# Where the weight parts begin in their buffers, in a decoder layer's matmuls

## The chip, the cores and the metric

The kernel runs on one core of a Trainium2 chip. Time is device time in microseconds for one execution; three runs gave 1137.29 to 1138.82 us, median 1138.13 us. A core has five engines that run their own instruction queues and meet at semaphores: TensorE (PE, with its weight loads shown as PEld), VectorE (DVE), ScalarE (ACT), GpSimd (POOL) and SyncE (SP), which issues most DMAs. SBUF is the memory on the chip that all of them read, with 128 partitions (rows); PSUM takes what TensorE computes.

## The reference

One layer of a decoder: 256 tokens, width 2,048, sixteen heads of 128 in two groups, an MLP of 8,192. All is float32.

```
h = rms_norm(x, norm1_g)
q_a, k_a, v_a, f_a, q_b, k_b, v_b = split(h @ w_in)          # 2048 x 6152
y_a = fox_attention(q_a, k_a, v_a, log_sigmoid(f_a + forget_b))
y_b = dilated_attention(q_b, k_b, v_b, rel_bias)
mixed = concatenate(rms_norm(y_a, outnorm_a_g), rms_norm(y_b, outnorm_b_g))
x = x + mixed @ w_out                                         # 2048 x 2048
h = rms_norm(x, norm2_g)
x = x + square(relu(h @ w_mlp_in)) @ w_mlp_out                # 2048 x 8192, 8192 x 2048
return rms_norm(x, final_norm_g)
```

## The kernel before

**Split operands.** A float32 value is kept as two parts of type float32r, hi (the value as ScalarE's copy rounds it) and lo (what remains, subtracted on VectorE). A product is three matmuls: hi by hi, hi by lo, lo by hi. Weights are split as they arrive (`split_rows`, L171 and L172), activations as they leave PSUM (`split_psum`, and L242/L243 with a gain).

**Chunks and steps.** All weights are cut into chunks of 512 columns: twelve for the projection ("q", "v", "k" of four groups of heads), eight for the output projection ("o", two kinds by four columns, each over 1,024 rows), and for each of four rounds four "u" (first MLP matrix) and four "d" (second). A chunk of 2,048 rows has 16 slots, one for each 128 rows (`kt`), and 8 steps of two slots. `load` brings 512 rows of a chunk by one DMA on SP into one of four `raw` buffers; a row of such a buffer has 520 elements, because one "v" chunk brings eight columns more, the forget gates. `split` makes the parts `whi` and `wlo` of one step, two times 512 columns in a buffer of their own, three steps (`LEAD`) before TensorE needs them; there are four buffers of each.

**Two ways of multiplying.** In `product` (L302 to L304; chunks q, k, v, o, d) 128 activation columns are the stationary operand, loaded by LDWEIGHTS, and 512 weight columns move past them. In `turned_product` (L316; chunks u) 128 weight columns are stationary and 256 activation columns (`aT_hi`, `aT_lo`) move. So each slot has six matmuls of 512 columns, or twelve of 256.

**The order** is written out by hand: a loop over all steps issues loads, splits and products, and `side` holds what else runs after each slot (drains, attention, norms). Each engine runs its own queue in that order. The places where buffers matter here:

- `wf` holds the two parts of the forget-gate weights of one step of the first "v" chunk. GpSimd makes them (L161, L162) when the step is split; TensorE uses them as the stationary operand of 16 columns at the end of each slot (L336). It has four buffers. In GpSimd's queue, between these, stands the power of the first norm (L264, called from `first_norm`), which VectorE needs for `rstdq`, by which the first query chunk is drained (L453 on ScalarE, L454 on VectorE) before its transposes (L466).
- `gate_h` is the decay of one head, made by GpSimd (L476) three slots before the head's scores (L493); heads follow each other every four slots. `sqt` holds the squares of a head's values (L547 on ScalarE), added up by GpSimd (L549). Both have two buffers.
- The last chunk has no `whi` and `wlo` for its first four steps: its parts go to `aT_hi` and `aT_lo`, whose activations have been used by then.

In SBUF, all buffers of `whi`, `wlo`, `aT_hi`, `aT_lo` and of the attention's and the MLP's activations begin at a multiple of 512 bytes, and every matmul's operand begins at a multiple of 512 bytes within them; only `wf` begins at multiples of 64.

Of the kernel before, what the change touches and what calls it, by code (L numbers as in the profile page):

```python
# [11 lines left out]
F32 = mybir.dt.float32  # L12
F32R = mybir.dt.float32r
# [6 lines left out]
P = 128  # L20
D_MODEL = 2048
SEQ = 256
TB = SEQ // P
HD = 128
NH = 8
D_GRP = NH * HD
D_FF = 4 * D_MODEL
KT = D_MODEL // P
CW = 512
# [7 lines left out]
QSCALE = HD ** -0.5  # L37

LEAD = 3
WARM, WARM2 = 8, 1  # L40


# [26 lines left out]
def kernel(  # L69
# [25 lines left out]
    one = ctx.enter_context(tc.tile_pool(name="one", bufs=1))  # L95
    two = ctx.enter_context(tc.tile_pool(name="two", bufs=2))
    wraw = ctx.enter_context(tc.tile_pool(name="wraw", bufs=4))
    wsplit = ctx.enter_context(tc.tile_pool(name="wsplit", bufs=LEAD + 1))
    few = ctx.enter_context(tc.tile_pool(name="few", bufs=1))
    psum = ctx.enter_context(tc.tile_pool(name="psum", bufs=2, space=PSUM))  # L100
    dram = ctx.enter_context(tc.tile_pool(name="dram", bufs=1, space=DRAM))
# [3 lines left out]
    chunks = []  # L105
# [27 lines left out]
    def load(i):  # L133
        if i >= len(steps) or steps[i][1] % 2 or (steps[i][0], steps[i][1] // 2) in raws:
            return
        ci, s = steps[i]
        _, _, w, r0, c0, cols, _ = chunks[ci]
        t = wraw.tile([P, 4, CW + NH], F32, name="raw")
        src = w[r0 + s * 256:r0 + s * 256 + 512, c0:c0 + cols].rearrange("(k p) c -> p k c", p=P)
        raws[ci, s // 2] = t  # L140
        if i == 0:
            return t, src
        n = 2 if i == 2 else 4
        for k in range(0, 4, n):
            nc.sync.dma_start(t[:, k:k + n, :cols], src[:, k:k + n])

    def split(i, j0=0, n=2):
        if i >= len(steps):
            return
        if j0:  # L150
            return split_rows(i, j0, n)
        ci, s = steps[i]
        t = raws[ci, s // 2][:, 2 * (s % 2):2 * (s % 2) + 2, :]
        if ci == len(chunks) - 1 and s < 4:
            hi, lo = (a[:, 4 * s:4 * s + 4, :].rearrange("p (k j) s -> p k (j s)", k=2) for a in (aT_hi, aT_lo))
        else:
            hi, lo = (wsplit.tile([P, 2, CW], F32R, name=n) for n in ("whi", "wlo"))
        if chunks[ci][5] > CW:
            f = wsplit.tile([P, 2, 2 * NH], F32R, name="wf")
            fh, fl = f[:, :, :NH], f[:, :, NH:]  # L160
            nc.gpsimd.tensor_copy(fh, t[:, :, CW:])  # L161
            nc.gpsimd.tensor_tensor(fl, t[:, :, CW:], fh.bitcast(F32), op=ALU.subtract)  # L162
            forget_w[i] = f
        splits[i] = (hi, lo)
        split_rows(i, j0, n)

    def split_rows(i, j, n):
        ci, s = steps[i]
        hi, lo = (a[:, j:j + n, :] for a in splits[i])
        t = raws[ci, s // 2][:, 2 * (s % 2) + j:2 * (s % 2) + j + n, :CW]  # L170
        nc.scalar.activation(hi, t, AF.Copy)  # L171
        nc.vector.tensor_tensor(lo, t, hi.bitcast(F32), op=ALU.subtract)  # L172
# [53 lines left out]
    gT = lead_in.tile([P, 96], F32, name="gT")[:, :48]  # L226
# [3 lines left out]
        nc.tensor.transpose(p[:, :k1], grow[:k1], ident[:k1, :k1])  # L230
        nc.vector.tensor_copy(gT[:, k0:k1], p[:, k0:k1])

    aT_hi = one.tile([P, KT, SEQ], F32R, name="aT_hi")
    aT_lo = one.tile([P, KT, SEQ], F32R, name="aT_lo")

    def split_psum(hi, lo, src, scale=None):

        if scale is None:
            nc.scalar.activation(hi, src, AF.Copy)  # L239
            nc.vector.tensor_tensor(lo, src, hi.bitcast(F32), op=ALU.subtract)  # L240
        else:
            nc.scalar.activation(hi, src, AF.Copy, scale=scale)  # L242
            nc.vector.scalar_tensor_tensor(  # L243
                lo, src, scale, hi.bitcast(F32), op0=ALU.mult, op1=ALU.subtract
            )

    def to_features(kt0, gain, n=2):

        p = psum.tile([P, 512], F32, name="tr")
        for j in range(n):  # L250
            for t in range(TB):
                c = (kt0 + j) * P
                nc.tensor.transpose(p[:, j * SEQ + t * P:j * SEQ + (t + 1) * P], xs[:, t, c:c + P], ident)  # L253
        for j in range(n):
            kt = kt0 + j
            split_psum(aT_hi[:, kt, :], aT_lo[:, kt, :], p[:, j * SEQ:(j + 1) * SEQ], gT[:, gain + kt:gain + kt + 1])

    def rsqrt(dst, ssq, n):

# [46 lines left out]
    def turned_product(ci, i, j, kt, kts):  # L306


        if kt == 0:
            accs[ci] = [psum.tile([P, CW], F32, name="acc", bufs=4) for _ in range(2)]  # L310
        hi, lo = splits[i]
        terms = ((hi, aT_hi), (hi, aT_lo), (lo, aT_hi))
        for b in range(4):
            acc = accs[ci][b // 2][:, b % 2 * SEQ:(b % 2 + 1) * SEQ]
            for n, (w, a) in enumerate(terms):
                nc.tensor.matmul(acc, w[:, j, b * P:(b + 1) * P], a[:, kt, :],  # L316
                                 start=kt == 0 and b % 2 == 0 and n == 0, stop=kt == kts - 1 and n == 2,
                                 skip_group_check=True)

    def products(i, j):  # L320
        ci, s = steps[i]
        what, key, _, _, _, cols, kts = chunks[ci]
        kt = 2 * s + j
        if what == "u":
            return turned_product(ci, i, j, kt, kts)
        if kt == 0:
            accs[ci] = [psum.tile([P, CW], F32, name="acc", bufs=4) for _ in range(TB)]
            if cols > CW:
                accs["f"] = psum.tile([P, 512], F32, name="sc")
        a = operands(what, key)  # L330
        go, end = kt == 0, kt == kts - 1
        for t in range(TB):
            product(accs[ci][t], a, kt, t, splits[i], j, slice(0, CW), go, end)
        if cols > CW:
            for n, part in enumerate(a[:2]):
                nc.tensor.matmul(accs["f"][:2 * NH, :SEQ], forget_w[i][:, j], part[:, kt, :],  # L336
                                 start=go and n == 0, stop=end and n == 1)
# [4 lines left out]
    def at(i, f, *a):  # L342
        side.setdefault(i, []).append((f, a))
# [128 lines left out]
    decay = {}  # L472

    def decay_of(hd):
        decay[hd] = two.tile([P, SEQ], F32R, name="gate_h")
        nc.gpsimd.tensor_scalar(  # L476
            decay[hd], gate_t.bitcast(F32), head[:, hd:hd + 1], 1.0, op0=ALU.mult, op1=ALU.mult
        )
# [50 lines left out]
    sq = [one.tile([P, SEQ], F32, name=f"sq{k}") for k in range(2)]  # L529
    seen = [0, 0]  # L530

    def values(g, h):
        half, kind = groups[g][3:]
        hd = kind * NH + half * 4 + h
        vh, vl = qkv[g, "v"]
        ph, pl = turned.pop((g, h))
        y = psum.tile([P, 512], F32, name="sc")
        terms = ((vh, ph), (vh, pl), (vl, ph))
        for t, c0, c1, o0 in ((0, 0, SEQ, 0), (1, SEQ, 3 * P, P)):
            for n, (v, p) in enumerate(terms):  # L540
                nc.tensor.matmul(  # L541
                    y[:, o0:SEQ], v[:, t, h * P:(h + 1) * P], p[:, c0:c1],
                    start=t == 0 and n == 0, stop=t == 1 and n == 2,
                )
        first = seen[kind] == 0
        s = sq[kind] if first else two.tile([P, SEQ], F32, name="sqt")
        nc.scalar.activation(s, y[:, :SEQ], AF.Square)  # L547
        if not first:
            nc.gpsimd.tensor_tensor(sq[kind], sq[kind], s, op=ALU.add)  # L549
        split_psum(yT_hi[:, hd, :], yT_lo[:, hd, :], y[:, :SEQ], gT[:, 32 + hd:33 + hd])  # L550
        seen[kind] += 1
# [126 lines left out]
    for ci, (what, key, *_rest) in enumerate(chunks[:-1]):  # L678
# [10 lines left out]
        elif what in "qk":  # L689
# [4 lines left out]
            if what == "k":  # L694
                kind = groups[key][4]
                for h in range(4):
                    n = e + 6 + 4 * h
# [20 lines left out]

    idle_products(WARM)
    split(0, 0, 1)  # L720
    gains(0, 16)
    to_features(0, 0, 1)
    split(0, 1, 1)
    to_features(1, 0, 1)
    idle_products(WARM2)
# [13 lines left out]
    at(21, nc.vector.tensor_copy, gcat, pk[:, :2 * P].rearrange("p (t s) -> p t s", t=TB))  # L739
    ahead = 2 * LEAD + 1  # L740

# [3 lines left out]
    for i in range(final):  # L745
        if i:
            load(i + ahead)
        for k in range(done + 1, upto.get(i, i + LEAD) + 1):
            split(k)
            load(k + LEAD + 2)  # L750
            done = k
# [34 lines left out]
```

## Time and profile before

| | |
|---|---|
| median of three runs | 1138.13 us |
| the profiled execution's own time | 1138.08 us |
| its span, first to last instruction | 1136.3 us |
| mean granted TensorE clock | 0.998 |
| bytes read from HBM | 205.93 MB, 183 GB/s over the span |
| first "u" chunk begins | 409 us |

The lines by which the time is read stand in the prediction. In a line of groups or of one source line, the name behind the operation is what it writes, the arrow, and what it reads; "128x256" is partitions by elements, "x1024" how many there were. Matmuls overlap: an instruction's duration holds its passage through the array, so the pace is read from starts, or from the length of a long row of them. L numbers are lines of the kernel before.

### The profile page before, as it was taken

The numbers are of one execution on the slowest core, as the hardware profiler recorded it, in microseconds if no ns is written. First come the engines' busy times: TensorE is split into PE (matmuls) and PEld (weight loads), VectorE is DVE, ScalarE is ACT, GpSimd is POOL, SyncE is SP. The second block draws the span as 40 slices with busy tenths as digits, with TensorE's granted clock in tenths as the row PEclk, the third lists the DMA queues.
The fourth block names the chain that finished last, engine by engine and source line by source line (L and its number), as shares of the span: only waits on it lengthen the run. The fifth ranks groups of instructions, "written<-read, shape, count | busy, mean of one in ns | idle before, by whom it ended". The sixth has DMA issues, their size and how long they took to land.

```text
span 1136.3 us, 16038 instructions
## 1 busy us (share of the span) xinstructions
PE 1124.0 (99%) x6635; PEld 993.6 (87%) x6635; DVE 639.5 (56%) x795; ACT 522.0 (46%) x675; POOL 32.2 (3%) x57
## 2 busy tenths in 40 slices
PE   8999999999999999999999999999999999999996
PEld 6778888888888899998889998889998889999886
DVE  5666656556576665555555555545555544555564
ACT  5545545445445554443334444343444333454451
POOL 0110201000001000000000000000000000000000
PEclk9999999999999999999999999999999999999999
DMA  8665454554544555556665555565555566546641
GB/s 310 223 203 168 149 186 148 185 186 149 186 149 168 169 186 184 182 172 210 201 196 178 185 182 196 185 189 182 169 203 187 194 200 190 181 161 202 242 148 74
DMA packets 104933, 209.08 MB, mean 184 GB/s; under 512 B 3651, under 2 KB 4508, under 8 KB 104732
## 3 DMA queue, kind: packets, MB, share of 16 engines
q1 hardware_dynamic: 104556, 207.00, 55.4%
q8 instruction: 52, 0.85, 0.3%
q0 software_dynamic: 304, 1.06, 0.3%
q14 instruction: 21, 0.17, 0.0%
HBM read 205.93 MB, written 2.11 MB: 183 GB/s over the span
## 4 chain that ended last, share of the span: by engine, by line
PE 98%; DMA 1%; DVE 0%; SPq 0%; ACT 0%; POOL 0%; issue 0%; DVEq 0%
PE acc L316 32%; PE acc L302 21%; PE acc L304 20%; PE acc L303 20%; PE sc L496 1%; PE sc L541 1%; PE tr L466 1%; DMA raw<-in_w_in_dram 1%; PE tr L253 1%; PE tr L523 0%; PE sc L336 0%; PE sc L493 0%; DVE wlo L172 0%; ACT whi L171 0%; DVE xs L649 0%; SPq L188 0%
## 5 line engine op out<-in xcount | busy, mean ns | idle before, releaser
L172 DVE TENSOR_TENSOR wlo<-raw,whi 128x1024 fp32r<-128x1024 f32 (+1 forms) x381 | 464.0, 1224 | 377.6 <-ACT whi L171 375.3
L171 ACT ACTIVATE whi<-raw 128x1024 fp32r<-128x1024 f32 (+1 forms) x381 | 399.7, 1055 | 407.4 <-PE acc L303 238.9
L316 PE MATMUL acc<-aT_hi,whi 128*128 128x256 f32 x1024 | 289.9, 283 | 0.0
L316 PE MATMUL acc<-aT_hi,wlo 128*128 128x256 f32 x1024 | 289.8, 283 | 0.0
L316 PE MATMUL acc<-aT_lo,whi 128*128 128x256 f32 x1024 | 289.8, 283 | 0.0
L302 PE MATMUL acc<-whi,big_hi 128*128 128x512 f32 (+1 forms) x632 | 245.7, 389 | 0.0
L304 PE MATMUL acc<-wlo,big_hi 128*128 128x512 f32 (+1 forms) x632 | 244.4, 387 | 0.0
L303 PE MATMUL acc<-whi,big_lo 128*128 128x512 f32 (+1 forms) x632 | 244.4, 387 | 0.0
L316 PEld LDWEIGHTS acc<-aT_lo,whi 128*128 128x128 f32 x1024 | 196.6, 192 | 0.2
L316 PEld LDWEIGHTS acc<-aT_hi,whi 128*128 128x128 f32 x1024 | 196.6, 192 | 0.2
L316 PEld LDWEIGHTS acc<-aT_hi,wlo 128*128 128x128 f32 x1024 | 196.6, 192 | 0.0
L302 PE MATMUL acc<-whi,aT_hi 128*128 128x512 f32 x384 | 154.6, 403 | 0.0
L304 PE MATMUL acc<-wlo,aT_hi 128*128 128x512 f32 x384 | 150.2, 391 | 0.0
L303 PE MATMUL acc<-whi,aT_lo 128*128 128x512 f32 x384 | 150.1, 391 | 0.0
L304 PEld LDWEIGHTS acc<-wlo,big_hi 128*128 128x128 f32 x632 | 118.7, 188 | 24.2
L302 PEld LDWEIGHTS acc<-whi,big_hi 128*128 128x128 f32 x632 | 118.8, 188 | 23.3
L303 PEld LDWEIGHTS acc<-whi,big_lo 128*128 128x128 f32 x632 | 118.8, 188 | 23.2
L304 PEld LDWEIGHTS acc<-wlo,aT_hi 128*128 128x128 f32 x384 | 72.1, 188 | 15.7
L302 PEld LDWEIGHTS acc<-whi,aT_hi 128*128 128x128 f32 x384 | 72.2, 188 | 13.8 <-ACT fu L383 0.6
L303 PEld LDWEIGHTS acc<-whi,aT_lo 128*128 128x128 f32 x384 | 72.4, 188 | 12.9 <-DVE aT_lo L243 0.3
L240 DVE TENSOR_TENSOR big_lo<-nat,big_hi 128x512 fp32r<-128x512 f32 x32 | 22.2, 693 | 22.3 <-ACT big_hi L239 22.3
L510 ACT ACTIVATE pr<-neg,st 128x128 f32<-128x128 f32 (+1 forms) x32 | 14.3, 449 | 40.1 <-DVE st L506 40.1
(160 smaller groups left out, 532.8 us busy)
## 6 DMA issues: line engine op xcount, KB each, us to landing
raw<-in_w_mlp_in_dram SPq DMA_DIRECT2D x64, 1024.0 KB, 5.4
raw<-in_w_mlp_out_dram SPq DMA_DIRECT2D x64, 1024.0 KB, 5.2
raw<-in_w_in_dram SPq DMA_DIRECT2D x42, 1024.0 KB, 5.1
raw<-in_w_out_dram SPq DMA_DIRECT2D x16, 1024.0 KB, 5.2
raw<-in_w_in_dram SPq DMA_DIRECT2D x4, 1040.0 KB, 5.2
raw<-in_w_in_dram SPq DMA_DIRECT2D x3, 512.0 KB, 8.4
xs<-in_x_dram SPq DMA_DIRECT2D x3, 512.0 KB, 9.5
big_lo<-rel_d POOLq DMA_DIRECT2D x1, 1024.0 KB, 7.0
```

Source lines behind the costliest of these rows:

```text
L171: nc.scalar.activation(hi, t, AF.Copy)
L172: nc.vector.tensor_tensor(lo, t, hi.bitcast(F32), op=ALU.subtract)
L240: nc.vector.tensor_tensor(lo, src, hi.bitcast(F32), op=ALU.subtract)
L253: nc.tensor.transpose(p[:, j * SEQ + t * P:j * SEQ + (t + 1) * P], xs[:, t, c:c + P], ident)
L302: nc.tensor.matmul(acc, xh, hi[:, j, cols], start=go, stop=False)
L303: nc.tensor.matmul(acc, xl, hi[:, j, cols], start=False, stop=False)
L304: nc.tensor.matmul(acc, xh, lo[:, j, cols], start=False, stop=end)
L316: nc.tensor.matmul(acc, w[:, j, b * P:(b + 1) * P], a[:, kt, :], start=kt == 0 and b % 2 == 0 and n == 0, stop=kt == kts - 1 and n == 2, s ...
L466: nc.tensor.transpose(p[:, j * SEQ + t * P:j * SEQ + (t + 1) * P], ts[t][:, h * P:(h + 1) * P], ident)
L496: nc.tensor.matmul(s[:, c0:c1], q[:, h, t * P:(t + 1) * P], k[:, h, :c1 - c0], start=n == 0 and kind == 1, stop=n == 2,)
L510: nc.scalar.activation(pr[:, c0:c1], neg[:, c0:c1], AF.Exp, bias=st[:, 0, t:t + 1], scale=-1.0, accum_out=st[:, 1, t:t + 1],)
L541: nc.tensor.matmul(y[:, o0:SEQ], v[:, t, h * P:(h + 1) * P], p[:, c0:c1], start=t == 0 and n == 0, stop=t == 1 and n == 2,)
```

## The change

1. The buffers of `whi` and `wlo` get 64 elements more (`LINE`, 256 bytes). The two parts of a step begin 0 to 56 elements into their buffers, in steps of 8 elements (32 bytes); `places` gives hi's and lo's place for each chunk. Of the twelve projection chunks, the first eight have both parts at 8 times the chunk's number, the last four at two places half a line apart. The "o" chunks have lo one step after hi. Of the "u" chunks, the first eight have both parts at the same place, the others half a line apart. The "d" chunks have hi at 16 elements times the round and lo at 16 times the chunk.
2. `aT_hi` and `aT_lo` get 64 elements more and move behind the weight buffers. The first norm's activations stay at their beginning; the second norm's, which the "u" chunks use, are written and read 8 elements (32 bytes) further on (`bT_hi`, `bT_lo`).
3. `wf` has two buffers instead of four, `gate_h` and `sqt` one instead of two. With this the rest fits in memory.

All buffers still begin at multiples of 256 bytes.

```diff
+LINE = 64
...
+    wide = ctx.enter_context(tc.tile_pool(name="wide", bufs=1))
...
+    def places(ci):
+
+        what, key = chunks[ci][:2]
+        if what == "u":
+            n = 4 * key[0] + key[1]
+            return (8 * n, 8 * n) if n < 8 else (8 * (n - 8), 8 * ((n - 4) % 8))
+        if what == "d":
+            return 16 * key[0], 16 * key[1]
+        n = 4 * key[0] + key[1] if what == "o" else ci
+        if what == "o":
+            return 8 * n, 8 * ((n + 1) % 8)
+        return (8 * n, 8 * n) if n < 8 else (8 * (2 * n - 15), 8 * ((2 * n - 11) % 8))
...
-            hi, lo = (wsplit.tile([P, 2, CW], F32R, name=n) for n in ("whi", "wlo"))
+            hi, lo = (
+                wsplit.tile([P, 2 * CW + LINE], F32R, name=n)[:, b:b + 2 * CW].rearrange("p (j c) -> p j c", j=2)
+                for n, b in zip(("whi", "wlo"), places(ci))
+            )
         if chunks[ci][5] > CW:
-            f = wsplit.tile([P, 2, 2 * NH], F32R, name="wf")
+            f = wsplit.tile([P, 2, 2 * NH], F32R, name="wf", bufs=2)
...
-    aT_hi = one.tile([P, KT, SEQ], F32R, name="aT_hi")
-    aT_lo = one.tile([P, KT, SEQ], F32R, name="aT_lo")
+    aT = {}
+    for n in ("hi", "lo"):
+        aT[n] = wide.tile([P, KT * SEQ + LINE], F32R, name="aT_" + n)
+
+    def features(b):
+        return (aT[n][:, b:b + KT * SEQ].rearrange("p (k s) -> p k s", k=KT) for n in ("hi", "lo"))
+
+    aT_hi, aT_lo = features(0)
+    bT_hi, bT_lo = features(8)
...
-            split_psum(aT_hi[:, kt, :], aT_lo[:, kt, :], p[:, j * SEQ:(j + 1) * SEQ], gT[:, gain + kt:gain + kt + 1])
+            fh, fl = (aT_hi, aT_lo) if gain == 0 else (bT_hi, bT_lo)
+            split_psum(fh[:, kt, :], fl[:, kt, :], p[:, j * SEQ:(j + 1) * SEQ], gT[:, gain + kt:gain + kt + 1])
...
-        terms = ((hi, aT_hi), (hi, aT_lo), (lo, aT_hi))
+        terms = ((hi, bT_hi), (hi, bT_lo), (lo, bT_hi))
...
-        decay[hd] = two.tile([P, SEQ], F32R, name="gate_h")
+        decay[hd] = two.tile([P, SEQ], F32R, name="gate_h", bufs=1)
...
-        s = sq[kind] if first else two.tile([P, SEQ], F32, name="sqt")
+        s = sq[kind] if first else two.tile([P, SEQ], F32, name="sqt", bufs=1)
```

No engine's instructions change their order. What changes is who waits. GpSimd's queue at the first "v" chunk, before: each pair L161, L162 makes the `wf` of one step, and in brackets stand the engines or queues waited for (Pool, PE, DVE, and DMAHW for a load).

```order
L161 CAST wf<-raw 128x2x8 [waits DMAHW5_49]
L162 TENSOR_TENSOR wf<-raw,wf 128x2x8 [waits Pool_49]
L161 CAST wf<-raw 128x2x8
L162 TENSOR_TENSOR wf<-raw,wf 128x2x8 [waits Pool_49]
L161 CAST wf<-raw 128x2x8 [waits DMAHW6_49]
L162 TENSOR_TENSOR wf<-raw,wf 128x2x8 [waits Pool_49]
L264 TENSOR_TENSOR rstd_123<-rs_v,half_t 128x2 [waits DVE_49]
L161 CAST wf<-raw 128x2x8
L162 TENSOR_TENSOR wf<-raw,wf 128x2x8 [waits Pool_49]
L161 CAST wf<-raw 128x2x8 [waits DMAHW6_49,PE_49]
```

The same place of GpSimd's queue in the changed kernel, where these lines are L179, L180 and L290:

```order
L179 CAST wf<-raw 128x2x8 [waits DMAHW5_49]
L180 TENSOR_TENSOR wf<-raw,wf 128x2x8 [waits Pool_49]
L179 CAST wf<-raw 128x2x8
L180 TENSOR_TENSOR wf<-raw,wf 128x2x8 [waits Pool_49]
L179 CAST wf<-raw 128x2x8 [waits DMAHW6_49,PE_49]
L180 TENSOR_TENSOR wf<-raw,wf 128x2x8 [waits Pool_49]
L290 TENSOR_TENSOR rstd_126<-rs_v,half_t 128x2 [waits DVE_49]
L179 CAST wf<-raw 128x2x8 [waits PE_49]
L180 TENSOR_TENSOR wf<-raw,wf 128x2x8 [waits Pool_49]
L179 CAST wf<-raw 128x2x8 [waits DMAHW6_49,PE_49]
```

The wait for TensorE has moved from the fifth pair to the third, which stands ahead of the power of the first norm.

## The prediction

> **What bounds the kernel now.** I read the page's busy shares first, then the chain that ended last in order of time, then the rows of the matmul lines, and last the few microseconds around the places where the change can make somebody wait.
>
> ```profile
> span 1136.3 us, 16038 instructions
> PE 1124.0 (99%) x6635; PEld 993.6 (87%) x6635; DVE 639.5 (56%) x795; ACT 522.0 (46%) x675; POOL 32.2 (3%) x57
> PE 98%; DMA 1%; DVE 0%; SPq 0%; ACT 0%; POOL 0%; issue 0%; DVEq 0%
> ```
>
> TensorE is busy for 99% of the span and is 98% of the chain. A busy PE need not be at its peak, so the next question is how far apart its matmuls start, which the chain in order of time tells.
>
> ```profile
> 414.58 87.84 PE acc L316 x732
> 589.49 92.15 PE acc L316 x768
> ```
>
> In the MLP's first product 768 matmuls of 256 columns take 92.15 us: 120.0 ns each. Between these two pieces (502.42 to 589.49 us) lie the 384 matmuls of 512 columns of one round of the MLP's second product: 87.07 us / 384 = 226.7 ns each. The two differ by 106.7 ns for 256 columns more, so a column costs 0.417 ns, and each matmul carries **13.3 ns** over its columns, the same at both widths. Over some 6,100 matmuls that is 81 us, the only sum here that a place in memory could change. The rows by line show how steady it is:
>
> ```profile
> L316 PEld LDWEIGHTS acc<-aT_lo,whi x1024: 187/192/192, 409.2 to 1039.6; 128*128 128x128 f32 x171
> L316 PE MATMUL acc<-aT_hi,whi x1024: 277/283/365, 409.2 to 1039.6; 128*128 128x256 f32 x171
> L316 PE MATMUL acc<-aT_lo,whi x1024: 279/283/283, 409.4 to 1039.7; 128*128 128x256 f32 x171
> ...
> L303 PEld LDWEIGHTS acc<-whi,big_lo x632: 187/188/192, 310.7 to 1127.3; 128*128 128x128 f32 x158
> L303 PE MATMUL acc<-whi,big_lo x632: 283/389/397, 310.9 to 1127.4; 128*128 128x512 f32 x154, 128*128 128x256 f32 x4
> L303 PE MATMUL acc<-whi,aT_lo x384: 387/389/496, 7.1 to 310.2; 128*128 128x512 f32 x192
> ```
>
> The three figures are minimum, median and maximum in ns. Two things matter. The median is nearly the maximum, although the weight buffers, the columns of a weight and the activation rows change from matmul to matmul; but all those starts are multiples of 512 bytes, so the rows say nothing of starts in between. And a weight load that lies wholly beside a matmul of 256 columns takes 192 ns, beside one of 512 columns 188: matmul and next load do touch each other a little.
>
> **Part one, the new starts.** Nothing is added or removed on TensorE: the same 6,635 loads and matmuls in the same order, reading hi and lo weights 0 to 224 bytes into their buffers and, in the first MLP product, activations 32 bytes in. The price per matmul is not in the trace, so it is bounded by the nearest rows. From below: the shortest L316 matmul is 277 against 283, the shortest L303 one of 512 columns 387 against 389, so at best -6 and -2 ns. From above: 397 against 389, so +8 ns at 512 columns (486 and 496 are first matmuls after other work, as is the 365); at 256 columns the third L316 row goes furthest:
>
> ```profile
> L316 PE MATMUL acc<-aT_hi,wlo x1024: 278/283/285, 409.5 to 1039.8; 128*128 128x256 f32 x171
> ```
>
> 285 against 283, so +2 ns. These extremes come with changed neighbours (other matmuls just before), not with other addresses.
>
> How many would be touched? Where weights are the moving side, the start relative to the activations changes for 11 of 12 projection chunks (1,056 matmuls), 336 of the 384 of the output projection and 1,152 of the 1,536 of the second MLP product: 2,544. In the first MLP product (3,072) the moving start changes for all, the distance between the two operands for all but 320 (both parts of one chunk, hi of another, also begin 32 bytes in): 2,752. The ends are then -(2,752 x 6 + 2,544 x 2) ns = **-21.6 us** and 3,072 x 2 + 2,544 x 8 ns = **+26.5 us**.
>
> I take **0** between these ends, by three rows. First, the 13.3 ns hardly depend on how much the next load reads:
>
> ```profile
> L336 PEld LDWEIGHTS sc<-aT_hi,wf x16: 94/94/95, 35.5 to 61.1; 128*16 128x16 f32 x16
> L336 PE MATMUL sc<-aT_lo,wf x16: 277/278/281, 35.8 to 61.4; 128*16 128x256 f32 x16
> ```
>
> The forget-gate weights have 16 columns instead of 128, yet the matmul's figure falls only from 283 to 278. Two readers colliding in memory should collide an eighth as often; a fixed cost of changing weights would look like this. (These weights also begin at steps of 64 bytes, and 277 to 281 is all their spread.) Second, other readers and writers of the same memory leave no mark:
>
> ```profile
> 412.00:500.00 88.00, 88.00 (x737) 88.00 (x736) 48.48 (x54) 40.29 (x47) 0.69 (x1) 1.00 0.55 181
> ```
>
> In these 88 us (PE, PEld, DVE, ACT, POOL, clock, DMA, GB/s) VectorE is busy for 48, ScalarE for 40, the DMA engines for 55%, and the matmuls still stand 120 ns apart. Third, in one step of 120 ns a matmul reads 256 columns (1,024 bytes a row) and the next load 128 (512 bytes): wherever the two start, they drift across 512 bytes of distance in each step, and a fixed shift moves a meeting rather than removes it.
>
> The Trainium skill weighs in here: "TensorE: Matmul & The Clock Gate", Part 2, step 1, gives TensorE two independent read ports and says "Loading the next tile's weights doesn't steal SBUF read bandwidth from the running matmul." By that rule the new starts give 0; the 192 against 188 ns above does not quite agree, so the ends stay open.
>
> ScalarE and VectorE now write at those starts too. They already read at uneven ones, as a raw row is 520 elements (2,080 bytes):
>
> ```profile
> L171 ACT ACTIVATE whi<-raw x381: 629/1060/1072, 4.5 to 1109.3; 128x1024 fp32r<-128x1024 f32 x190, 128x512 fp32r<-128x512 f32 x1
> L172 DVE TENSOR_TENSOR wlo<-raw,whi x381: 692/1226/1951, 5.2 to 1110.5; 128x1024 fp32r<-128x1024 f32 x190, 128x512 fp32r<-128x512 f32 x1
> ```
>
> Median and maximum of L171 are 1% apart over all those starts, so I price the writes at 0. If they cost 10%, the cover is VectorE's 56%: nothing shows on the path.
>
> **Part two, fewer buffers.** gate_h and sqt go to one buffer. Their next writer comes four slots later (rows 6 us apart), so 0:
>
> ```profile
> 129.12 0.80 POOL L549 TENSOR_TENSOR sq<-sq,sqt 128x256 f32<-128x256 f32 x1 [5.75 <-ACT sqt L547]
> 135.35 0.74 POOL L549 TENSOR_TENSOR sq<-sq,sqt 128x256 f32<-128x256 f32 x1 [5.43 <-ACT sqt L547]
> ```
>
> GpSimd waits over 5 us before each 0.8 us of work; that is the cover.
>
> wf goes from four buffers to two, and this **adds a wait**: the third pair of wf operations may start only when TensorE has used the first wf. Behind that pair in GpSimd's queue stands the power for the first norm (L264), for which VectorE waits, with its weight splits and the first query's drain behind it.
>
> ```profile
> 27.09 0.25 POOL L161 CAST wf<-raw 128x16 fp32r<-128x16 f32 x1 [1.76 <-DMA raw<-in_w_in_dram]
> 36.36 0.72 POOL L264 TENSOR_TENSOR rstd<-rs_v,half_t 128x2 f32<-128x2 f32 x1 [8.71 <-DVE rs_v L263]
> 37.82 0.20 POOL L161 CAST wf<-raw 128x16 fp32r<-128x16 f32 x1 [0.26 <-PE sc L336]
> 38.09 1.20 POOL L162 TENSOR_TENSOR wf<-raw,wf 128x16 fp32r<-128x16 f32 x1
> 41.34 0.22 POOL L162 TENSOR_TENSOR wf<-raw,wf 128x16 fp32r<-128x16 f32 x1
> ...
> 37.11 0.16 DVE L265 TENSOR_TENSOR rs_t<-rstd 128x2 f32<-128x2 f32 x1 [0.84 <-POOL rstd L264]
> 40.30 0.74 DVE L454 TENSOR_SCALAR nat<-acc,rstdq 128x512 f32<-128x512 f32 x1
> ...
> 42.45 0.60 PE L466 MATMUL tr<-ident,nat 128*128 128x128 f32 x4
> ```
>
> The cast at 37.82 waited, with four buffers, for just that first wf's last use; with two, the cast of 27.09 waits for it. So: cast 37.82, subtraction 38.09 + 0.22 = 38.31, power until 39.05, and L265 at about 39.15 instead of 37.11: VectorE is 2.0 us late. Its splits are made three steps ahead, a step being 12 matmuls of 226.7 ns and more, so 8 us cover them. The query drain ends at 41.04 + 2.0 = 43.05, while TensorE comes for it at 42.45: **+0.6 us** on the path, with 0 and 2.0 as ends. Raw buffers come free up to 7 us later there, but loads land in 5.2 us and were waited for only twice on ScalarE:
>
> ```profile
> ACT whi L171 <- DMA raw<-in_w_in_dram: 4.2, 2, 2.3
> ```
>
> The subtraction at 38.09 took 1.20 us while VectorE ran its splits, the one at 41.34, beside none, 0.22; VectorE now stands still at that moment, so I take 0.22; with 1.20 the stall would be 1.6 us. The Trainium skill, "SBUF — State Buffer", Who interferes with whom, has a VectorE instruction with two SBUF inputs block a GpSimd one that reads SBUF; these two rows agree, and by it the small value holds here.
>
> **Sum.** The profiled execution took 1138.08 us around its span of 1136.3; the median is 1138.13, the same within 0.05. 1138.1 + 0 + 0.6 = **1138.7 us**.
>
> **Rivals.** *Faster: load and matmul collide because all starts are equal modulo 512.* For it: 192 against 188 ns, and 277 against 283 where the rhythm is broken. Against it: the 16-column row. At most -21.6 us; with half the places out of step, -10.8 + 0.6: **1127.9 us**.
>
> *Slower: a moving row that begins off a boundary needs one fetch more.* All moving starts are now even, so no row excludes it. I take it to strike starts at odd steps of 32 bytes: 768 projection and 192 output matmuls at +8 ns, 3,072 of the first MLP product at +2: 7.7 + 6.1 = 13.8 us, **1152.5 us**. It decides from about 0.4 ns per matmul: 2.3 us over 5,600.
>
> *The starts do nothing and the wf wait costs its full 2.0 us*: 1140.1, still inside the first case's bounds.
>
> **How the numbers follow.** A change within 0.2% (2.3 us) is about what a measurement of this kernel cannot tell from none. No dependence on the start, with the small wait: 0.52. Collisions lifted: 0.26. Extra fetches: 0.22. The low end, 1121, covers three quarters of the largest gain; the high end, 1153, takes in the slower case as priced; what lies past both is under 2 in 10.
>
> **What would show it.** If I am right, L316 stays at 283 and L303 at 389 in every chunk, the long L316 pieces of the chain stay at 92.15 us, and the L466 transposes near 42.5 us wait some 0.6 us for L454's line. If starts matter, pieces of the chain differ by chunk: shorter for the faster rival; longer at odd starts, with the second MLP product unchanged, for the slower one. Matmul rows that move in every chunk alike would make my reading of the 13.3 ns wrong.

## The result, and the profile after

The changed kernel takes **1144.39 us** (median of four runs, 1144.05 to 1144.53), the kernel before 1137.86 us in the four runs beside it. The ratio is 1.0056, with a 95% interval of 1.0039 to 1.0074: **slower by 6.5 us**. That is inside the predicted range, but the likeliest case, no change at 1138.7 us, is not what happened.

The page after, with the span, the busy shares, and the chain's shares:

```profile
span 1142.8 us, 16028 instructions
PE 1130.9 (99%) x6635; PEld 989.1 (87%) x6635; DVE 640.1 (56%) x795; ACT 522.0 (46%) x675; POOL 32.2 (3%) x57
PE 98%; DMA 1%; DVE 1%; SPq 0%; ACT 0%; POOL 0%; issue 0%; DVEq 0%
```

The number of matmuls and loads is the same and the chain is still TensorE's; TensorE is busy 6.9 us longer. So the time went into the pace of the matmuls. The chain in order of time splits it by stage. First the pieces of before that the prediction didn't show (start us, us, what), then those of after:

```profile
409.41 2.88 PE acc L316 x24
...
768.71 92.15 PE acc L316 x768
947.92 92.15 PE acc L316 x768
```

```profile
415.89 2.81 PE acc L342 x24
...
420.98 86.57 PE acc L342 x732
595.77 90.62 PE acc L342 x768
775.15 90.24 PE acc L342 x768
953.84 91.43 PE acc L342 x768
```

L342 is L316 of before, the first MLP product. Read both the lengths and the gaps between the pieces:

| stage | before, us | after, us | difference |
|---|---|---|---|
| up to the first MLP product (projection, attention, output projection) | 409.41 | 415.89 | +6.48 |
| first MLP product, the four long pieces | 364.29 | 358.86 | -5.43 |
| second MLP product, the three gaps between those pieces | 87.07, 87.07, 87.06 | 88.22, 88.76, 88.45 | +4.23 |
| from the last long piece to the end of the span | 96.23 | 97.53 | +1.30 |

Together with the 0.08 us that the start of the first round became shorter, this is the 6.5 us. (About half a microsecond of the first row is the beginning of the kernel: the first product starts at 7.13 us after and at 6.59 before, and between 6.43 and 7.13 us in all the kernels here.) Two large effects of opposite sign nearly cancel: where weights are the moving operand (512 columns), matmuls became slower; where activations are (256 columns), faster.

The windows show that it goes by chunk, as each chunk has its own places. Four stretches of 20 us of after, each inside one chunk: the second MLP product at places 0, 0 (hi, lo, in elements) and 0, 16; the first at 48, 48 and 56, 56. The number in the first brackets counts the matmuls that overlap the stretch:

```profile
509.00:529.00 20.00, 20.00 (x90) 16.57 (x89) 11.77 (x12) 9.25 (x10) 0.00 (x0) 1.00 0.54 180
531.00:551.00 20.00, 20.00 (x88) 16.16 (x87) 9.10 (x9) 7.43 (x7) 0.00 (x0) 1.00 0.59 179
643.00:663.00 20.00, 20.00 (x169) 20.00 (x168) 10.65 (x11) 9.29 (x10) 0.00 (x0) 1.00 0.51 163
666.00:686.00 20.00, 20.00 (x178) 20.00 (x178) 11.58 (x11) 9.59 (x11) 0.00 (x0) 1.00 0.54 177
```

At one granted clock (the 1.00) the 512-column matmuls run 90 or 88 to a stretch, the 256-column ones 169 or 178. From the recorded starts in these chunks: 226.7, 232.0, 120.0 and 113.3 ns a matmul. The first and the last are steady, every start like the one before (once the chunk has settled). The other two are means of a pattern that repeats: starts 224 to 241 ns apart, again after 15 matmuls, and 116 to 125 ns apart, again after six. Over all chunks, 256-column matmuls run at 113.3 to 121.1 ns (120.0 everywhere before), those of the second MLP product at 226.67 where both operands begin at the same place and 228.9 to 234.2 elsewhere.

The rows by line answer to those of before:

```profile
L342 PE MATMUL acc<-aT_hi,whi x1024: 276/281/363, 415.7 to 1044.7; 128*128 128x256 f32 x171
L342 PE MATMUL acc<-aT_lo,whi x1024: 274/281/300, 415.8 to 1044.9; 128*128 128x256 f32 x171
...
L328 PE MATMUL acc<-whi,big_hi x632: 276/392/483, 315.8 to 1133.7; 128*128 128x512 f32 x154, 128*128 128x256 f32 x4
```

Medians of 281 and 392 ns instead of 283 and 389: a matmul's own duration shows the change, but smaller than the pace does.

### The profile page after: what moved, and what is told of

Its sections match the earlier page's. It is cut to its first block, busy times and chain, and to the rows that moved or that the text cites. A ratio compares the mean times of both kernels' runs of the same rounds, so it can differ in the third digit from the quotient of the medians.

```text
span 1142.8 us, 16028 instructions
## 1 busy us (share of the span) xinstructions
PE 1130.9 (99%) x6635; PEld 989.1 (87%) x6635; DVE 640.1 (56%) x795; ACT 522.0 (46%) x675; POOL 32.2 (3%) x57
## 4 chain that ended last, share of the span: by engine, by line
PE 98%; DMA 1%; DVE 1%; SPq 0%; ACT 0%; POOL 0%; issue 0%; DVEq 0%
PE acc L342 32%; PE acc L328 21%; PE acc L329 21%; PE acc L330 21%; PE sc L522 1%; PE sc L567 1%; PE tr L492 1%; DMA raw<-in_w_in_dram 1%; PE tr L278 1%; PE tr L549 0%; PE sc L362 0%; DVE wlo L190 0%; PE sc L519 0%; ACT whi L189 0%; DVE xs L675 0%; SPq L206 0%
## 5 line engine op out<-in xcount | busy, mean ns | idle before, releaser
L342 PE MATMUL acc<-aT_lo,whi 128*128 128x256 f32 x1024 | 287.8, 281 | 0.0
L342 PE MATMUL acc<-aT_hi,whi 128*128 128x256 f32 x1024 | 287.5, 281 | 0.0
L342 PE MATMUL acc<-aT_hi,wlo 128*128 128x256 f32 x1024 | 287.4, 281 | 0.0
L342 PEld LDWEIGHTS acc<-aT_lo,whi 128*128 128x128 f32 x1024 | 193.1, 189 | 0.2
L342 PEld LDWEIGHTS acc<-aT_hi,whi 128*128 128x128 f32 x1024 | 193.1, 189 | 0.2
L342 PEld LDWEIGHTS acc<-aT_hi,wlo 128*128 128x128 f32 x1024 | 193.2, 189 | 0.0
L328 PEld LDWEIGHTS acc<-whi,big_hi 128*128 128x128 f32 x632 | 118.8, 188 | 25.7
```

Source lines behind the costliest of these rows:

```text
L328: nc.tensor.matmul(acc, xh, hi[:, j, cols], start=go, stop=False)
```

## The experiments

**Distance** below is the weights' place less the activations' place, in bytes modulo 256. A **pace** is the mean time from one matmul's start to the next. Each run is compared with the kernel before on the same chip. The expectations call the kernels e1 to e12, in the order in which they stand here. The theories: A, the pace depends on the distance between the two operands; B, on each operand's own start (the prediction's extra fetch).

### Everything but the places

```diff
     def places(ci):
-        what, key = chunks[ci][:2]
...
+        return 0, 0
...
-    bT_hi, bT_lo = features(8)
+    bT_hi, bT_lo = features(0)
```

> The changed kernel with all starts even again (both weight parts at the beginning of their buffers, second activations at 0), but with its buffers, their order in memory and two wf, one gate_h, one sqt buffer kept. Theory A (the matmuls' pace follows the distance in memory between the row a matmul reads and the weights loaded beside it): all chunks are back at 226.7 and 120.0 ns, only the wf wait is left, +0.4 us (the gap of the changed kernel's L492 transposes, 0.50 us between starts where 0.11 is usual): 1138.3 us. Theory C (the buffers' new sizes and order, or the new waits, cost it): 1142 to 1144.4 us stays.

1138.91 us against 1138.61 (ratio 1.0005, 0.9996 to 1.0014); L332, its line for the first MLP product, shows pieces of 87.84 and three times 92.15 us, those of the kernel before. What the places leave is the `wf` wait. In its timeline TensorE's transposes of the first query chunk are parted:

```profile
42.36 0.27 PE L482 MATMUL tr<-ident,nat 128*128 128x128 f32 x1
42.89 0.55 PE L482 MATMUL tr<-ident,nat 128*128 128x128 f32 x3 [0.26 <-DVE nat L470]
```

The second starts 0.53 us after the first. The four in before's row take 0.60 us together and the first alone 0.27 here, so 0.11 apart is usual, and the wait costs 0.42 us. All else of the 6.5 us lies in the places.

### Another distance alone, and the same distance elsewhere

In before, with nothing but the second norm's activations 64 bytes further on (distance 192 in the first MLP product):

```diff
...
+    aT_hi, aT_lo = features(0)
+    bT_hi, bT_lo = features(16)
...
+            fh, fl = (aT_hi, aT_lo) if gain == 0 else (bT_hi, bT_lo)
...
-        terms = ((hi, aT_hi), (hi, aT_lo), (lo, aT_hi))
+        terms = ((hi, bT_hi), (hi, bT_lo), (lo, bT_hi))
```

> The kernel before, with one thing changed: the second norm's activations, which move in the first MLP product, are written and read 64 bytes further on; weights, buffers and waits as before. That is the distance of the changed kernel's chunk (1,3), whose weights begin 224 bytes in and its activations 32. Theory A: 113.3 instead of 120.0 ns on 3,072 matmuls, -20.5 us, 1117.5 us. Theory B (a start of its own, not the distance, sets the pace: of the weights at 224 bytes, or of moving rows off even places): nothing gained, 1138 us, or slower.

1131.77 us against 1138.61 (0.9943, 0.9930 to 0.9955). All sixteen chunks changed alike, but to 117.8 ns, not to 113.3:

```profile
414.27 86.22 PE acc L322 x732
587.56 90.45 PE acc L322 x768
```

The other kernel moves everything by 32 bytes, weights, both norms' activations and the attention's and MLP's, so that no distance changes:

```diff
+        return 8, 8
...
-    aT_hi, aT_lo = features(0)
+    aT_hi, aT_lo = features(8)
...
-    yT_hi = one.tile([P, 2 * NH, SEQ], F32R, name="big_hi")
...
+        one.tile([P, 2 * NH * SEQ + LINE], F32R, name="big_" + n)[:, 8:8 + 2 * NH * SEQ].rearrange("p (k s) -> p k s", s=SEQ)
```

> The changed kernel with every start of these matmuls 32 bytes in: weight parts, both norms' activations, and the attention's and MLP's activations (big_hi, big_lo). No start is even, but all distances are those of the kernel before. Theory A: 226.7 and 120.0 ns again, 1138.5 us. Theory B, in which a moving row off an even place needs more: the matmuls of 512 columns stay near 232 to 234 ns, some +15 us and more.

1139.34 us (1.0009, 1.0000 to 1.0019), and the pieces are 87.84 and three times 92.15 us again. **Theory B falls**: an odd 32-byte start costs a matmul nothing by itself; the distance does.

### The distance in steps of 16 bytes

```diff
+        n = 4 * (4 * key[0] + key[1]) if what in "ud" else 0
+        return n, n
...
-    bT_hi, bT_lo = features(8)
+    bT_hi, bT_lo = features(0)
```

> A survey: the changed kernel with both parts at 16 bytes times the number of the chunk (0 to 240) in the sixteen chunks of each MLP product, 0 elsewhere, second activations at 0. Read by chunk, not by its total. Theory A: in the first product the steps depend on the distance modulo 256 bytes or less, 120.0 at 0 and near 113.3 at 192 (64 bytes behind the activations); in the second, 226.7 at 0 and 229 to 234 elsewhere, unless odd multiples of 16 bytes do something new. Theory B: the first product, whose moving rows are even in all chunks, stays at 120 in all of them.

1140.46 us, one run. The pace by chunk, from the recorded starts, to about 0.1 ns:

| distance, bytes | 0 | 16 | 32 | 48 | 64 | 80 | 96 | 112 | 128 | 192 | 208 | 240 |
|---|---|---|---|---|---|---|---|---|---|---|---|---|
| 256 columns, ns | 120.0 | 118.3 | 118.3 | 117.8 | 113.3 | 118.8 | 117.3 | 120.0 | 118.6 | 117.8 | 116.7 | 117.3 |
| 512 columns, ns | 226.7 | 231.6 | 233.4 | 233.3 | 228.9 | 231.1 | 233.4 | 231.1 | 233.3 | 233.3 | 234.6 | - |

The four distances left out (144, 160, 176 and 224) have 116.7 to 120.0 and 231.1 to 234.3 ns. The windows of 20 us of the first product at distances 64 and 192:

```profile
591.00:611.00 20.00, 20.00 (x179) 20.00 (x178) 9.31 (x9) 7.88 (x8) 0.00 (x0) 1.00 0.59 179
951.00:971.00 20.00, 20.00 (x172) 20.00 (x171) 8.85 (x8) 7.52 (x8) 0.00 (x0) 1.00 0.57 176
```

The expected 113.3 ns at distance 192 came at 64 instead, while the changed kernel's chunk at 56, 56 (its activations at 8, so 192) had 113.33. One distance, two paces: at 256 columns distance alone isn't the whole cause, and the 256-column row of the table holds only for the order in which these chunks follow each other. That 128 differs from 0 (233.3 against 226.7 ns at 512 columns), while weight buffers that lie at 0 and at 256 modulo 512 in turn (each is 4,352 bytes, 17 times 256) run alike, makes the period 256 bytes.

At 512 columns the changed kernel shows the distance at work inside one chunk. In its last one the parts of the first four steps lie in `aT_hi` and `aT_lo`, at distance 0, those of the other steps at 192. Its 512-column matmuls start 226.7 ns apart in the former, after eight matmuls in which they settle, and 233.3 ns apart from the first one at 192 on.

### The two halves of the change

The first MLP product's places alone, all others even; then all others alone, with that product at distance 0:

```diff
+        n = 4 * key[0] + key[1] if what == "u" else None
+        if n is None:
+            return 0, 0
```

> The changed kernel with its places in the first MLP product alone; weight parts of all other chunks at the beginning of their buffers. If the two halves of the change add up: 1138.9 (all starts even) minus the 5.5 us that the first product's 16 chunks lost in the changed kernel's trace = 1133.4 us. If the first product's pace was a consequence of the other chunks' places (a chunk starts in the rhythm that the one before left), its gain comes out different, between 0 and 20 us.

```diff
         if what == "u":
-            n = 4 * key[0] + key[1]
-            return (8 * n, 8 * n) if n < 8 else (8 * (n - 8), 8 * ((n - 4) % 8))
+            return 8, 8
```

> The changed kernel with its places in all chunks but those of the first MLP product, whose weights begin 32 bytes in as their activations do (distance 0). First product 120.0 ns throughout; the rest as in the changed kernel: 1138.9 + 11.2 = 1150 us (11.7 us is what those chunks gained in the trace, less some 0.5 us of wait that the even kernel has as well). If the halves depend on each other, 1145 to 1155.

1133.66 us against 1138.38 (0.9953, 0.9937 to 0.9970), and 1150.22 us (1.0102, 1.0087 to 1.0117). Each holds the one small wait; -4.7 and +11.8 us less one wait of some 0.4 make +6.7, and the whole change gave +6.5. The change's parts are **one gain and one loss that add up**. The first of the two kernels has a detail: its chunk at 56, 56 ran at 117.77 ns, in the changed kernel at 113.33, with the same places in the whole round and only the 512-column chunks before it different.

### One distance, two paces

All sixteen chunks of the first MLP product at 56, 56 with activations at 8 (distance 192), and all at 16, 16 with activations at 0 (distance 64):

```diff
+        return (56, 56) if chunks[ci][0] == "u" else (0, 0)
```

```diff
+        return (16, 16) if chunks[ci][0] == "u" else (0, 0)
...
+    bT_hi, bT_lo = features(0)
```

> The changed kernel with all first-product chunks at the place of its chunk (1,3), 224 bytes in, activations 32 in, all other chunks even: a distance of 64 bytes modulo 256, that of e2, entered in the same rhythm of 226.7 ns. If the distance and the rhythm at entry set the pace: 117.8 ns in all 16 chunks, as in e2, about 1132.2 us. If the place itself gave that chunk its 113.3 ns: 113.3 in all of them, 1118.5 us.

> The same with the weights 64 bytes in and the activations at 0: the distance at which the survey's chunk (1,0) ran at 113.3 ns and the changed kernel's (0,3) at 117.8. If the rhythm at entry decides between these two, all 16 chunks, which are entered alike, have one of the two paces, the same in each round: 113.3 gives 1118.5 us, 117.8 gives 1132.2.

1121.89 and 1128.68 us, one run each. The first round's opening and the first two long pieces of either chain, distance 192 first:

```profile
410.09 2.73 PE acc L332 x24
...
415.11 86.22 PE acc L332 x732
588.41 87.05 PE acc L332 x768
```

```profile
410.04 2.83 PE acc L332 x24
...
415.13 82.98 PE acc L332 x732
585.17 90.45 PE acc L332 x768
```

Divided by their counts: 113.8, 117.8 and 113.3 ns at distance 192; 117.9, 113.4 and 117.8 ns at distance 64; the later rounds repeat the last value. Neither expectation is met whole, since both paces occur in one kernel at one distance. They occur even in one chunk, with the same places throughout: the first round opens with 24 matmuls at the pace of the later rounds, then transposes of the second norm break in twice, and the rest of the round keeps the other pace. So a pace, once taken, holds, here for rounds of 768 matmuls, until other work breaks in.

Nor is it enough to know which chunks ran ahead. The kernel with 64 bytes on the activations (e2) has the same distance of 192 and the same even 512-column chunks ahead of its later rounds, and those ran at 117.8 ns. The recorded starts differ at the seam: from the last 512-column matmul to the first of the next round it is 235 ns in e7 and 226 in e2.

### The best places found

Each round gets the distance at which it ran at 113.3 ns: 64 in the first, 192 in the others.

```diff
+        if what != "u":
+            return 0, 0
+        return (24, 24) if key[0] == 0 else (56, 56)
```

> Every part buffer begins at its even place, except those of the first MLP product: there the first round stands 64 bytes behind the place of the activations (the distance at which round 0 of e8_u_16 ran at 113.33 ns), rounds 1 to 3 stand 64 bytes ahead of it (the distance at which they ran at 113.33 ns in e7_u_56). Theory (distance, and the rhythm in which a chunk is entered, which each round repeats): all sixteen chunks at 113.33 ns, chain pieces of about 83.0 and three times 87.05 us, 1138.9 - 16 x 192 x 6.67 ns = 1118.4 us. Rival (the entry of round 1 depends on the rhythm that round 0 left): one or more rounds at 117.8 ns, each 3.4 us more, so 1121.8 to 1132.

**1118.82 us** against 1138.34 (0.9828, 0.9814 to 0.9841), 0.4 us from what was expected. Here is the page's line of engines, the chain and a row by line:

```profile
PE 1105.6 (99%) x6635; PEld 974.7 (87%) x6635; DVE 638.2 (57%) x795; ACT 522.2 (47%) x675; POOL 32.5 (3%) x57
```

```profile
414.76 82.98 PE acc L335 x732
584.85 87.04 PE acc L335 x768
```

```profile
L335 PE MATMUL acc<-aT_lo,whi x1024: 276/276/283, 409.7 to 1019.8; 128*128 128x256 f32 x171
```

From the recorded starts all chunks are at 113.3 ns, the first one once the second norm's transposes are done. This version beats both kernels, by 19.5 us the one before.

The same with the second MLP product in steps of 8 bytes:

```diff
+        n = 2 * (4 * key[0] + key[1]) if what == "d" else 0
+        return n, n
```

> As e9_two_places, and in the second MLP product chunk n = 4 x round + column stands 8 x n bytes behind the even place (0 to 120 bytes). Theory: distance 0 is the best place for these 512-column matmuls, so every other chunk shows more than 226.67 ns, 229 to 234, and the time is 15 chunks x 96 matmuls x 2.3 to 7.5 ns = 3 to 11 us over e9_two_places. Rival: some distance that is no multiple of 16 bytes gives these matmuls the gain that 64 bytes give the 256-column ones, 6.67 ns less, so a chunk at 220.0 ns.

1137.06 us, one run. No 512-column chunk came below 226.67 ns; the others show 229.0 to 235.5, and the seven distances that the survey has too (16 to 112 bytes) agree with it within 0.1 ns once settled. By the chain the second MLP product takes 7.6 us more, which is inside what was expected. But that is only part of the 18 us:

```profile
415.78 82.98 PE acc L336 x732
587.62 90.45 PE acc L336 x768
```

The first round keeps its 82.98 us; the three others, with their own places untouched, fell back to 117.8 ns, 3 x 3.41 = 10.2 us. Only the 512-column chunks ahead of them differ; at the seams it is now 231 to 233 ns instead of 235. So **how a chunk is entered decides between its two paces**.

### How much of the next load it takes

All places even (distance 0, by the edit of e1), with narrower weight loads in the first MLP product:

```diff
+            m = P if kt == 0 else 16
             for n, (w, a) in enumerate(terms):
-                nc.tensor.matmul(acc, w[:, j, b * P:(b + 1) * P], a[:, kt, :],
+                nc.tensor.matmul(acc[:m], w[:, j, b * P:b * P + m], a[:, kt, :],
```

> As e1_even (all places even, distance 0), but in the first MLP product every weight load after a chunk's first slot takes 16 columns of the 128, so those 2,880 matmuls leave out 112 of their 128 output rows. Theory (the part of the 13.3 ns that a place can remove is the matmul and the load beside it getting in each other's way): with an eighth of the load the matmuls run at 113.3 to 114.2 ns though the distance is 0, and the time is 1138.9 - 2,880 x 5.8 to 6.7 ns = 1119.7 to 1122.1 us. Rival, the first reason of the prediction (a fixed cost of changing weights, whatever the load reads): 120.0 ns and 1138.9 us.

> As e11_load16 with 64 of the 128 columns loaded, so those matmuls leave out 64 of their 128 output rows. Theory: what remains of the removable 6.67 ns follows the load's length, about half of it: 116 to 117.5 ns, 1127 to 1132 us. Rival (fixed cost): 120.0 ns and 1138.9 us. A second form of the theory (a meeting at the load's beginning only, whatever its length): 120.0 ns here and in e11_load16 too.

1119.95 us with 16 columns, 1120.56 us with 64, against 1138.19 (0.9839, 0.9811 to 0.9868; 0.9845, 0.9816 to 0.9873). The groups by line and form, 16 columns first, then 64 with one round's piece of its chain (in the groups: busy us, mean ns of one, idle before):

```profile
L333 PE MATMUL acc<-aT_hi,whi 128*16 128x256 f32 x960 | 265.2, 276 | 0.0
L333 PEld LDWEIGHTS acc<-aT_hi,whi 128*16 128x16 f32 x960 | 90.3, 94 | 18.2
...
L333 PE MATMUL acc<-aT_lo,whi 128*128 128x256 f32 x64 | 18.1, 283 | 0.0
```

```profile
585.19 87.38 PE acc L333 x768
...
L333 PE MATMUL acc<-aT_hi,whi 128*64 128x256 f32 x960 | 265.2, 276 | 0.0
L333 PEld LDWEIGHTS acc<-aT_hi,whi 128*64 128x64 f32 x960 | 128.7, 134 | 0.0
```

In one round 48 matmuls keep the full load. At 120.0 ns they take 5.76 us of the 87.38; the other 720 have 81.62 us, 113.4 ns each. A matmul beside a narrow load takes 276 ns even at distance 0, beside a full one 283, in the same kernel. So 6.7 ns of the 13.3 go with the width of the load, and 6.7 don't.

The edit narrows each matmul's output along with its load, which is a rival. The seams between full and narrow matmuls speak for the load: by the records, the last full matmul of a chunk, beside a load that is narrow already, takes 279 ns instead of 283, and the last narrow one, beside the next chunk's full load, 277 to 278 instead of 276. And at the best places full matmuls beside full loads run at 113.3 ns too. How the 6.7 ns divide, no run shows.

The expectation for 64 columns, that about half of the 6.67 ns stay, was wrong: 64 columns already leave nothing of it.

## Why the prediction was right or wrong

**The time lies in the range partly by luck.** 1144.39 us is between 1121 and 1153 because a gain of 5.4 us and a loss of 11.6 us nearly cancel; no case of the prediction had both, and the likeliest one, no dependence on the start, is refuted.

**The bound was right.** TensorE's matmul pace sets the end, and what moved, 6.5 us, moved in what each matmul carries over its columns, apart from the wait of 0.4 us and some half a microsecond at the start.

**Part one's term was wrong in its step "I take 0 between these ends".** It measured -5.4 us in the first MLP product and +11.6 us elsewhere (6.48 less the wait of 0.42, plus 4.23 and 1.30). Over 3,072 and 2,544 matmuls that is -1.8 and +4.6 ns each. The two ends of the sum held. Their counts are a little high: lo of one more "u" chunk begins 32 bytes in, and half of the last chunk keeps its distance, so 2,688 and 2,496 matmuls change theirs, and the ends are -21.1 and +26.1 us. Their prices are a little narrow: -6.67 ns instead of -6 in the best chunks of 256 columns, up to +8.9 instead of +8 ns at 512 columns in the steps of 8 bytes. (The low end of the range, 1121, covers 17.7 of the 21.6 us, four fifths and not three quarters.) The three reasons for 0 fell one by one. For the first, this line of before belongs beside those that the prediction shows:

```profile
L336 PE MATMUL sc<-aT_hi,wf x16: 278/279/281, 35.7 to 61.3; 128*16 128x256 f32 x16
```

- *The 16-column row as a sign of a fixed cost.* I misread it twice. The load that lies beside a matmul is that of the next matmul, and after `sc<-aT_lo,wf` comes a full load of the next slot: the one at 35.85 us starts together with a load of L302 that takes 0.19 us. The matmul with the narrow load beside it is the other one, `sc<-aT_hi,wf`, in the line above. Both come alone among matmuls of 512 columns, so neither shows a steady pace, and 278 beside 279 ns could not decide. And I set the 4 or 5 ns that they are below 283 against the whole 13.3; but the best places leave a matmul at 276 ns, so they were most of the 7 ns that can go. In the kernels with narrow loads 283 becomes 276.
- *Other readers and writers leave no mark.* That held, also at 113.3 ns (the window at distance 64 has the DMA engines at 59%), and says nothing of TensorE's own two reads.
- *A fixed shift moves a meeting rather than removes it.* Steps repeat, each like the last (every 120.0 or 113.3 ns) or in a short pattern, so whatever drift they hold comes again and again and doesn't average the places out. A shift changes what meets in all of them: with 64 bytes on the activations alone, all chunks went from 120.0 to 117.8 ns.

The sentence that the prediction quoted of the Trainium skill, "TensorE: Matmul & The Clock Gate", Part 2, step 1, that loading the next weights takes no read bandwidth from the running matmul, isn't borne out here: at distance 0 a 256-column matmul runs at 120.0 ns with a full load and at 113.4 ns with a narrow one.

**Written starts and single buffers at 0 were right.** The kernel with even places keeps the single buffers and shows 1138.91 us for 1138.61, no more than the `wf` wait. The splits' medians after are 1060 and 1225 ns, where the prediction's rows have 1060 and 1226:

```profile
L189 ACT ACTIVATE whi<-raw x381: 619/1060/1068, 4.7 to 1115.8; 128x1024 fp32r<-128x1024 f32 x190, 128x512 fp32r<-128x512 f32 x1
L190 DVE TENSOR_TENSOR wlo<-raw,whi x381: 691/1225/1864, 5.4 to 1117.0; 128x1024 fp32r<-128x1024 f32 x190, 128x512 fp32r<-128x512 f32 x1
```

**The wf wait was right, and 0.2 us too large**: 0.42 for 0.6. The timeline of the kernel with even places has each step of its chain:

```profile
37.73 0.20 POOL L169 CAST wf<-raw 128x16 fp32r<-128x16 f32 x1 [12.86 <-PE sc L352]
38.00 0.22 POOL L170 TENSOR_TENSOR wf<-raw,wf 128x16 fp32r<-128x16 f32 x1
38.18 0.72 POOL L280 TENSOR_TENSOR rstd<-rs_v,half_t 128x2 f32<-128x2 f32 x1
38.94 0.16 DVE L281 TENSOR_TENSOR rs_t<-rstd 128x2 f32<-128x2 f32 x1 [2.75 <-POOL rstd L280]
...
42.09 0.74 DVE L470 TENSOR_SCALAR nat<-acc,rstdq 128x512 f32<-128x512 f32 x1
```

The cast waits for the first `wf`, the subtraction takes the small value, VectorE goes on at 38.94 where 39.15 was worked out, and the drain ends at 42.83 for 43.05. The Trainium skill's rule in "SBUF — State Buffer", Who interferes with whom, by which the small value held, agrees with 0.22 us beside an idle VectorE.

**The rivals.** The faster one had the mechanism that the narrow loads speak for, load and matmul in each other's way at distance 0, and twice its size: I priced -10.8 us, and the first MLP product gave -5.4. It had no place for the other sign, distance 0 as the *best* for 512 columns. The slower one had the sign, and its mechanism fell: starts at odd steps cost nothing when the distance stays, and the second MLP product, which it left alone at even steps, lost 5.5 us. Of what was to show it, "pieces of the chain differ by chunk" came true.

What stays open: what the two reads contend for, why the period is 256 bytes, why 512 columns want distance 0 and 256 columns don't, and what in the entry chooses the pace. Narrow loads beside 512-column matmuls weren't tried, nor narrow loads with a full output.

## What to carry to other kernels

Where matmuls with a weight load each set the end, work out the pace from starts and set it beside the columns; if it carries more than the best pace of its shape, shift one operand (here by 64 bytes modulo 256) and measure each shape apart, since what helps one may hurt the other. Keep the shift to the shape that gains, and look at the pace round by round: the same places may hold two paces. A time for the whole kernel hides this: the change here had a gain of 5 us in it and looked like a plain loss.

## What the hardware showed that was not expected

- The pace of a float32r matmul with a 128-column load beside it depends on the distance of the two operands modulo 256 bytes, and the two widths want opposite things: at distance 0, 256 columns run at 120.0 ns, near their slowest, and 512 columns at 226.67, their fastest.
- At distances 64 and 192, 256 columns have two lasting paces, 113.3 and 117.8 ns, each held over 768 matmuls. How the row of matmuls is entered chooses: transposes in the middle of a chunk switched it, and so did other places in the 512-column chunks ahead. At distance 0 all rounds settled at 120.0 ns, also behind the 512-column chunks of the changed kernel.
- At distance 0, matmuls of 256 columns with loads of 128 columns take 6.7 ns more than those with loads of 64 or 16 columns (and as many output rows), though the loads of 64 and 16 still take 134 and 94 ns.
